# Second attention of a two-layer decoder: the causal mask by GpSimd's selection, and another order of weight preparation and transposes

## Chip, cores and metric

The kernel runs on one core of a Trainium2 chip. The metric is the device time of one execution in microseconds (us). TensorE (PE in the profile) multiplies matrices, VectorE (DVE) and ScalarE (ACT) do elementwise work, GpSimd (POOL) does small jobs, and SyncE (SP) issues the DMAs. A whole run is one launch.

## What is computed

Two decoder layers on 256 tokens of width 1024, in float32. The first layer's mixer is a dilated window attention, the second's is a forgetting attention; each mixer is followed by a SwiGLU layer of width 2816. The change lies in the second mixer:

```python
def forgetting_mixer(h, w_in, b_f, w_out):
    proj = h @ w_in
    q, k, v = ...                      # 16 heads of 64
    log_f = jax.nn.log_sigmoid(proj[..., 3 * ATTN_WIDTH:] + b_f)
    c = lax.cumsum(log_f, axis=1)
    def block(args):                   # 128 queries at a time
        s = jnp.einsum('bihd,bjhd->bhij', qi, k) * scale
        s = s + ci[..., None] - ck[:, :, None, :]
        s = jnp.where(key_pos[None, :] <= qpos[:, None], s, NEG_INF)
        p = jax.nn.softmax(s, axis=-1)
        return jnp.einsum('bhij,bjhd->bihd', p, vf)
    ...
    return o @ w_out
```

## The kernel before

Every weight matrix is streamed from HBM in pieces of 128 x 2048, and used in two parts so that products keep float32 accuracy: a high part `wh` (ScalarE copies the loaded half piece `raw` to a shorter type, L79) and a low part `wl` (VectorE subtracts `wh` from `raw`, L83). Each product is three matmuls (`mm3`, L202 and L207): high times high, high times low, low times high. `raw` has five buffers of half a piece, used in turn, so SyncE can issue a load only when the subtraction five half pieces earlier has read its buffer. `wh` and `wl` have four buffers each. `weights` (L153) is called by the step that uses a piece, and makes the pieces up to two steps ahead.

The second attention (L904 to L974) goes through the twelve pieces of its input projection, in the order of `b_units` (L137). The text calls the i-th of them unit i: units 0 to 2 are values, 3 and 4 are q and k of head group 0, 5 and 6 of group 1, 7 and 8 of group 2, 9 and 10 of group 3, and 11 is the values of group 3. A head group is four heads, worked on as two pairs. Between the units stand the steps of the attention, by a table `due` of times: half numbers mean in the middle of a unit.

- `bias` (L846): loads the rows of cumulated log gates for a pair into all partitions (L849) and adds the causal mask to the two diagonal blocks of each head on GpSimd (L851).
- `scores_b` (L857): q times k on PE into four PSUM banks (L864), then VectorE adds the bias and takes the maximum (L876), ScalarE takes exponentials and their sums (L878), VectorE the reciprocal (L883), and both scale the probabilities `p` (L885 ScalarE, L886 VectorE). In it `release` emits low parts that were held back for units 3 and 5.
- `trans_b` (L889): twelve transposes of `p` on PE (L298) into three PSUM banks, and three copies of these to SBUF on VectorE (L303).
- `pv_b` (L896): values times transposed `p` on PE (L310), then the split of the result into `oth` and `otl`, the high and low part of the attention's output.

For group 0 scores come after unit 5, transposes in the middle of unit 7, values and the scores of group 1 at the end of unit 7's projection. Groups 1 and 2 follow two and four units later, with transposes in the middle of units 9 and 11. Group 3 has its scores at the end of unit 11, and its transposes and values inside the output projection.

`out_proj` (L630) multiplies the attention's output by `b_out`, first for the first 128 tokens (t = 0): for each pair of n (two halves of the width) and k (eight slices) three matmuls, called a piece here. Slices k = 6 and 7 are those of group 3. With `done` = 5 the pieces of slices 0 to 4 are put around the steps that are still due.

Each engine works through its instructions in one order that is fixed when the program is built, from the order of the code, with `first()` (L43) moving an instruction ahead and `issue_after` keeping one behind another. An engine waits at an instruction whose inputs or buffers aren't there, and all that is behind it waits too.

Of the kernel before, what the change touches and what calls it, by code (L numbers as in the profile page):

```python
# [10 lines left out]
F32 = mybir.dt.float32  # L11
F32R = mybir.dt.float32r
AF = mybir.ActivationFunctionType
ALU = mybir.AluOpType
AX = mybir.AxisListType

P = 128
D = 1024
S = 256
KT = D // P  # L20
# [7 lines left out]
NEG = -1e30  # L28
# [3 lines left out]
def trunk(ctx: ExitStack, tc: tile.TileContext, T, out):  # L32
    nc = tc.nc

    cst = ctx.enter_context(tc.tile_pool(name="cst", bufs=1))
# [23 lines left out]
    def const(name, shape):  # L59
        c = cst.tile(shape, F32, name=name)  # L60
        nc.sync.dma_start(c, T[name])
        return c
# [90 lines left out]
    def weights(nm, i, after=None, ahead=AHEAD, hold=None):  # L153

        upto = order.index((nm, i)) + ahead
        while state["next"] <= min(upto, len(order) - 1):
            key = order[state["next"]]
            cuts = []
            ready[key] = piece(key, cuts)
            for cut in cuts:  # L160
                cut(after, hold)
            state["next"] += 1
        return ready.pop((nm, i))
# [91 lines left out]
    def v_tile(o=None, r=None):  # L255

        v = ap.tile([P, 512], F32, tag="v", name="v", bufs=7)
        with first():
            if r:
                for t in range(2):  # L260
                    s = slice(t * S, (t + 1) * S)
                    nc.scalar.activation(v[:, s], o[:, s], AF.Copy, scale=r[t])
            elif o is not None:
                nc.scalar.activation(v, o, AF.Copy)
        return v
# [24 lines left out]
    def masked(s, sc, mask):  # L290
        with first():
            nc.vector.scalar_tensor_tensor(s, sc, HD ** -0.5, mask, op0=ALU.mult, op1=ALU.add)

    def transposed(blocks, copy=nc.vector.tensor_copy, tag="tr", home="pt"):

        tr = psum(tag)
        for i, b in enumerate(blocks):
            nc.tensor.transpose(tr[:, i * P:(i + 1) * P], b, ident)  # L298
        n = len(blocks) * P
        bufs, cols = {"pt": (3, 512), "bias": (4, 6 * P)}[home]  # L300
        w = ap.tile([P, cols], F32, tag=home, name="pt", bufs=bufs)
        with first():
            copy(w[:, :n], tr[:, :n])  # L303
        return w

    def pv(o, v, kb, pr, w, n, start, stop):
# [21 lines left out]
    for i, c in enumerate(room):  # L328
        b = 1 + (i > 1)
        n = S + 512  # L330
# [17 lines left out]
    xt = xt_tile()  # L348
# [15 lines left out]
    part = [sums[:, :S], sums[:, S:512], sums[:, 512:], sqs[:, :512], sqs[:, 512:]]  # L364
# [8 lines left out]
    for k in range(KT):  # L373
        if k % 4 == 0:
            w = tuple(wp.tile([P, 2048], F32R, tag=y, name=y, bufs=4) for y in ("wh", "wl"))
# [49 lines left out]
    x = []  # L425

    ot = fm_tile("ot", KT, 1)
# [102 lines left out]
    due = {}  # L530
# [5 lines left out]
    for i, (hq, g, w) in enumerate(a_units):  # L536
# [15 lines left out]
        if i in (24, 31):  # L552
            x.append(hrow("x"))
            t = len(x) - 1
# [72 lines left out]
                parts.append(sq(hn[:, s]))  # L627
        return hn, parts

    def out_proj(nm, ot, h, grow, done, banks):  # L630

        ws = [weights(nm, i) for i in range(4)]
        xt = xt_tile()
        res = []

        def part(t, acc, nk):
            last = None
            for n, k in nk:
                c = (k % 2) * D + n * 512
                last = mm3(acc[n], both(ot, ALL, k, slice(t * P, (t + 1) * P)),  # L640
                           both(ws[k // 2], ALL, slice(c, c + 512)), k == 0, k == KT - 1)
            return last

        def cols(ks):
            return [(n, k) for n in range(2) for k in ks]

        for t in range(2):
            acc = [psum(banks[t]) for _ in range(2)]
            if t == 0:

                nk = cols(range(done))
                last = part(t, acc, nk[:done])
                nk = nk[done:]
                per = -(-len(nk) // (len(due) - 1))
                for i in sorted(due):
                    with tc.issue_after(last.ins):
                        for fn, a in due[i]:
                            fn(*a)
                    last = part(t, acc, nk[:per]) or last
                    nk = nk[per:]  # L660
                due.clear()
                part(t, acc, nk)
                last = part(t, acc, cols(range(done, KT)))
            else:
                part(t, acc, cols(range(2)))
                with tc.issue_after(last.ins):
                    part(t, acc, cols(range(2, 6)))
                    norm_t(*res[0], grow, xt, 0)
                    part(t, acc, cols(range(6, KT)))
            res.append(residual(acc, h[t], f"h_{nm}{t}"))  # L670
        return res, xt
# [110 lines left out]
        return res  # L782

    g_f = load_grow(1)
    hs, xt = out_proj("a_out", ot, x, g_f, 6, ("sc", "mm"))
    causal = const("causal", [P, P])
    bf = cst.tile([P, NH], F32, name="bf")
    nc.sync.dma_start(bf, T["bf"].partition_broadcast(P))
    wf32 = const("b_f_in", [P, KT * NH]).rearrange("p (k c) -> p k c", k=KT)
# [36 lines left out]
    behind = []  # L826
# [19 lines left out]
    def bias(hq, pr):  # L846

        b = ap.tile([P, 6 * P], F32, tag="bias", name="bias", bufs=4)
        nc.sync.dma_start(b, sums[hq * 4 + pr * 2:hq * 4 + pr * 2 + 2].rearrange("h c -> (h c)").partition_broadcast(P))  # L849
        d = b.rearrange("p (h b j) -> p h b j", h=2, b=3)[:, :, 0:3:2]  # L850
        nc.gpsimd.tensor_tensor(d, d, causal[:, None, None, :].to_broadcast([P, 2, 2, P]), op=ALU.add)  # L851
        bq[hq]["bias", pr] = b

    ot = fm_tile("ot", KT, 1)
# [80 lines left out]
    for i, (hq, w) in enumerate(b_units):  # L935
        if i < 3:
            continue
        wt = weights("b_in", hq * 3 + w, behind if i in (3, 5) else None, hold=held)
        o = psum("mm")
        if w < 2:  # L940
            for c in range(2):
                proj_feat(xt, wt, o[:, c * S:(c + 1) * S], c)
                if c == 0:
                    for fn, a in due.pop(i - 0.5, ()):
                        fn(*a)
            if w == 0:

                for fn, a in due.pop(i, ()):
                    fn(*a)
            bq[hq][w] = ap.tile([P, 2, S], F32, tag=f"fm{w}", name=f"fb{w}", bufs=2)  # L950
            with first():
                held = nc.scalar.activation(bq[hq][w], o.rearrange("p (a b) -> p a b", a=2), AF.Copy,
                                            scale=(0.125, 1.0)[w])
            if w == 1:
                j = i + 1

                later(j, scores_b, hq)
                if hq < 2:
                    for pr in range(2):
                        later(j + 1, bias, hq + 2, pr)  # L960
                later(j + 1.5, trans_b, hq)
                for pr in range(2):
                    later(j + 2, pv_b, hq, pr)
        else:
            for t in range(2):
                proj_tok(xt, wt, o[:, t * S:(t + 1) * S], t)
                if t == 0:
                    for fn, a in due.pop(i - 0.5, ()):
                        fn(*a)
            bq[hq][w] = v_tile(o)  # L970
        for fn, a in due.pop(i, ()):
            fn(*a)
    g_f = load_grow(3)
    hs, xt = out_proj("b_out", ot, [h for h, _ in hs], g_f, 5, ("mm", "sc"))  # L974

    def finish(t, h, parts):
        r = rstd(parts)
# [41 lines left out]
def _constants():  # L1019

    pos = np.arange(S)
    perm = np.array([P * b + 4 * u + a for b in range(2) for a in range(4) for u in range(32)])
    half = ROT // 2
    inv = np.power(np.float32(500000.0), -np.arange(half, dtype=np.float32) * np.float32(2.0) / np.float32(ROT))
    ang = (pos[:, None].astype(np.float32) * inv[None, :].astype(np.float32)).astype(np.float32)
    cos, sin = np.cos(ang)[perm], np.sin(ang)[perm]
    lay = lambda a, fill: np.ascontiguousarray(np.tile(np.concatenate(
        [a.T, np.full((HD - ROT, S), fill)]), (2, 1)).astype(np.float32))
    rcos = lay(np.concatenate([cos, cos], 1), 1.0)
    rsin = lay(np.concatenate([-sin, sin], 1), 0.0)  # L1030
    d = perm[:, None] - perm[None, :]
    bias = lambda ok: np.where(ok, 0.0, NEG).astype(np.float32)
    m0 = bias((d >= 0) & (d <= 128))
    m0 = np.concatenate([m0[:P, :P], m0[P:]], 1)

    res = np.concatenate([np.arange(32), P + np.arange(32)])
    own = np.tile(d[res][:, res].reshape(2, 1, 32, 64), (1, 4, 1, 1)).reshape(2, P, 64)
    m1 = bias((own >= 0) & (own % 4 == 0) & (own <= 512))
    m2 = bias((own >= 0) & (own % 16 == 0) & (own <= 2048))
    m12 = np.stack([m1, m2], 2).transpose(1, 0, 2, 3).reshape(P, S)  # L1040
    causal = bias(pos[:P, None] >= pos[None, :P])
    return perm, {
        "ident": np.eye(P, dtype=np.float32), "rcos": rcos, "rsin": rsin,
        "mask0": m0, "mask12": m12,
        "causal": causal,
    }


# [57 lines left out]
```

## Time and profile before

| | |
|---|---|
| time, three runs | 745.35, 745.67, 746.33 us; median 745.67 us |
| profiled execution | 749.27 us, of which the span of the trace is 747.5 us |
| mean granted TensorE clock | 0.994 |
| DVE, ACT, POOL busy | 66%, 50%, 9% of the span |
| moved by DMA | 138.07 MB, 185 GB/s |
| second attention, units 3 to 11 and the output projection | about 463 to 560 us of the span |

The trace is one execution. A row of the timeline gives the start in us, the length in us, the engine, the line of the kernel, the operation with output and inputs, the count, and in brackets how long the engine had been idle and what released it. A row of the chain gives start, length and what ran there; the chain is followed back from the program's last instruction. In the rows of one line the three numbers are the shortest, the median and the longest duration in ns. Matmuls overlap: their spacing, not their length, is the time that they take on PE.

### The profile page before, as it was taken

What the parts mean: (1) busy time and instruction counts of PE and PEld (TensorE: products, weight loads), DVE (VectorE), ACT (ScalarE), POOL (GpSimd) and SP (SyncE); (2) the same over time, 40 slices, a digit from 0 to 9 for tenths busy, and PEclk for the clock granted to TensorE, in tenths of its full rate; (3) what the DMA queues carried; (4) which work ended last, traced back from release to release, by engine and by line L of the source; (5) the groups of instructions that cost most, each with busy time, mean ns of one, the idle gap of its engine ahead of it and who ended that gap; (6) DMA issues with size and microseconds to landing.
All of it is one profiled execution on the core that took longest, in us unless ns stands there. A gap on an engine that the chain in (4) does not pass through costs nothing.

```text
span 747.5 us, 14342 instructions
## 1 busy us (share of the span) xinstructions
PE 737.5 (99%) x5916; PEld 680.5 (91%) x5916; DVE 492.6 (66%) x768; ACT 375.7 (50%) x617; POOL 66.8 (9%) x98
## 2 busy tenths in 40 slices
PE   9999999999999999999999999999999999999996
PEld 7999989999988789999999988979789999999995
DVE  6997987787888575545455474686767545456533
ACT  7536437437436565344454453576555444444521
POOL 0600003005005000000000004211000000000001
PEclk9999999999999999999999999999999999999998
DMA  8865544644646267565667452874537665656601
GB/s 330 298 203 171 177 155 151 203 159 153 209 144 222 82 229 238 191 200 179 202 204 241 138 168 87 288 243 146 171 105 221 231 198 180 202 189 215 209 1 56
DMA packets 39441, 138.07 MB, mean 185 GB/s; under 512 B 4528, under 2 KB 5840, under 8 KB 39376
## 3 DMA queue, kind: packets, MB, share of 16 engines
q1 hardware_dynamic: 39232, 137.01, 55.3%
q8 instruction: 46, 0.75, 0.4%
q14 instruction: 19, 0.16, 0.1%
q10 hardware_dynamic: 144, 0.15, 0.1%
HBM read 136.07 MB, written 1.07 MB: 183 GB/s over the span
## 4 chain that ended last, share of the span: by engine, by line
PE 90%; ACT 3%; DMA 3%; DVE 2%; issue 1%; SPq 0%; POOL 0%; POOLq 0%; DVEq 0%; ACTq 0%
PE ps_mm L207 31%; PE ps_mm L202 16%; PE ps_tr L207 9%; PE ps_sc L207 8%; PE ps_o L207 7%; PE ps_tr L202 5%; PE ps_sc L202 4%; PE ps_o L202 4%; PE ps_o L310 2%; DMA raw<-in_b_in 2%; DVE wl L83 1%; DMA otl<-in_lead 1%; PE ps_tr L298 1%; ACT wh L79 1%; PE ps_sc L473 1%; ACT p L878 1%
## 5 line engine op out<-in xcount | busy, mean ns | idle before, releaser
L79 ACT ACTIVATE wh<-raw 128x1024 fp32r<-128x1024 f32 x236 | 243.2, 1055 | 240.4 <-PE ps_tr L207 66.5
L83 DVE TENSOR_TENSOR wl<-raw,wh 128x1024 fp32r<-128x1024 f32 x236 | 288.5, 1242 | 88.1 <-ACT wh L79 87.8
L202 PE MATMUL ps_mm<-xt,wh 128*128 128x256 f32 x816 | 228.2, 280 | 0.0
L207 PE MATMUL ps_mm<-xt,wl 128*128 128x256 f32 x816 | 226.8, 278 | 0.1
L207 PE MATMUL ps_mm<-xt,wh 128*128 128x256 f32 x816 | 226.6, 278 | 0.0
L202 PEld LDWEIGHTS ps_mm<-xt,wh 128*128 128x128 f32 x816 | 153.9, 189 | 1.8 <-issue 1.7
L207 PEld LDWEIGHTS ps_mm<-xt,wl 128*128 128x128 f32 x816 | 153.4, 188 | 0.5 <-DVE wl L83 0.5
L207 PEld LDWEIGHTS ps_mm<-xt,wh 128*128 128x128 f32 x816 | 153.4, 188 | 0.0
L207 PE MATMUL ps_tr<-xt,wl 128*128 128x256 f32 x304 | 83.8, 276 | 0.0
L207 PE MATMUL ps_tr<-xt,wh 128*128 128x256 f32 x304 | 83.8, 276 | 0.0
L202 PE MATMUL ps_tr<-xt,wh 128*128 128x256 f32 x304 | 83.6, 276 | 0.0
L702 DVE TENSOR_TENSOR sa<-ps_tr,sa 128x256 f32<-128x256 f32 x38 | 16.1, 424 | 73.9 <-PE ps_tr L207 73.8
L207 PEld LDWEIGHTS ps_tr<-xt,wh 128*128 128x128 f32 x304 | 57.1, 188 | 0.0
L207 PEld LDWEIGHTS ps_tr<-xt,wl 128*128 128x128 f32 x304 | 57.1, 188 | 0.0
L202 PEld LDWEIGHTS ps_tr<-xt,wh 128*128 128x128 f32 x304 | 56.9, 188 | 0.0
L284 POOL COPY v<-v 32x256 f32<-32x256 f32 x64 | 38.0, 594 | 176.1 <-ACT v L280 173.4
L202 PE MATMUL ps_mm<-wh,xt 128*128 128x512 f32 (+1 forms) x144 | 49.8, 346 | 0.0
L207 PE MATMUL ps_mm<-wl,xt 128*128 128x512 f32 (+1 forms) x149 | 49.1, 335 | 0.0
L207 PE MATMUL ps_mm<-wh,xt 128*128 128x512 f32 (+1 forms) x149 | 49.1, 335 | 0.0
L172 POOL TENSOR_SCALAR rs<-ssq 128x1 f32<-128x1 f32 x7 | 2.1, 303 | 422.8 <-ACT junk L181 422.8
L202 PE MATMUL ps_sc<-wh,ah 128*128 128x512 f32 x80 | 31.4, 392 | 0.0
L207 PE MATMUL ps_sc<-wl,ah 128*128 128x512 f32 (+1 forms) x82 | 31.3, 385 | 0.0
(230 smaller groups left out, 1103.3 us busy)
## 6 DMA issues: line engine op xcount, KB each, us to landing
raw<-in_gu SPq DMA_DIRECT2D x88, 512.0 KB, 4.8
raw<-in_a_in SPq DMA_DIRECT2D x68, 512.0 KB, 4.6
raw<-in_dn SPq DMA_DIRECT2D x44, 512.0 KB, 4.6
raw<-in_b_in SPq DMA_DIRECT2D x24, 512.0 KB, 4.7
raw<-in_a_out SPq DMA_DIRECT2D x8, 512.0 KB, 5.3
raw<-in_b_out SPq DMA_DIRECT2D x8, 512.0 KB, 4.9
bias<-sums SPq DMA_DIRECT2D x8, 384.0 KB, 6.1
grow<-in_norms SPq DMA_DIRECT2D x4, 512.0 KB, 5.9
```

Of the source, the lines that this page charges most:

```text
L79: a = nc.scalar.activation(view(hi), src, AF.Copy)
L83: return nc.vector.tensor_tensor(view(lo), src, view(hi).bitcast(F32), op=ALU.subtract)
L172: nc.gpsimd.tensor_scalar(m, s, rest, None, op0=ALU.add)
L202: nc.tensor.matmul(o, sh, mh, start=start, stop=False)
L207: last = nc.tensor.matmul(o[:, u], s, m[:, u], start=False, stop=end and u.stop == n)
L284: nc.gpsimd.tensor_copy(v[1 + a % 2][n:n + 32, a // 2 * S:a // 2 * S + S], by_t[a * 32:a * 32 + 32, t, g])
L298: nc.tensor.transpose(tr[:, i * P:(i + 1) * P], b, ident)
L310: nc.tensor.matmul(o[h * HD:(h + 1) * HD], v[:, c:c + HD], w(h), start=start, stop=stop)
L473: nc.tensor.matmul(sc[h][c, o:o + 64], q[HR[h], pr, qb * P + a * 32:qb * P + a * 32 + 32], k[HR[h], pr].rearrange("p (b n) -> p b n", b=2) ...
L702: nc.vector.tensor_tensor(a, u, sg, op=ALU.mult)
L878: nc.scalar.activation(s[:, u], s[:, u], AF.Exp, bias=nm[:, j:j + 1], scale=-1.0, accum_out=den[:, j:j + 1])
```

## The change

Three edits. The mask of the diagonal blocks is made by GpSimd's `affine_select`, which keeps an element where row minus column is at least 0 and writes -1e30 elsewhere, two instructions for a pair's bias (one for each block of 128 queries) in place of one addition; the constant `causal` and its load are gone, and an unused tile keeps its place. In units 7, 9 and 11, in the middle of which a group is transposed, the low parts of the pieces made there (two half pieces each) are emitted behind the group's last copy. And in the output projection `out_proj` puts nine pieces of slices 0 to 5 ahead of the last transposes, where five of slices 0 to 4 stood.

```diff
+    copied = {}
+
     def transposed(blocks, copy=nc.vector.tensor_copy, tag="tr", home="pt"):
...
         with first():
-            copy(w[:, :n], tr[:, :n])
+            copied["last"] = copy(w[:, :n], tr[:, :n])
         return w
...
-    def out_proj(nm, ot, h, grow, done, banks):
+    def out_proj(nm, ot, h, grow, ks, done, banks):
...
-                nk = cols(range(done))
+                nk = cols(range(ks))
                 last = part(t, acc, nk[:done])
                 nk = nk[done:]
...
-                last = part(t, acc, cols(range(done, KT)))
+                last = part(t, acc, cols(range(ks, KT)))
...
-    hs, xt = out_proj("a_out", ot, x, g_f, 6, ("sc", "mm"))
-    causal = const("causal", [P, P])
+    hs, xt = out_proj("a_out", ot, x, g_f, 6, 6, ("sc", "mm"))
+    cst.tile([P, P], F32, name="gap")
...
         d = b.rearrange("p (h b j) -> p h b j", h=2, b=3)[:, :, 0:3:2]
-        nc.gpsimd.tensor_tensor(d, d, causal[:, None, None, :].to_broadcast([P, 2, 2, P]), op=ALU.add)
+        for e in range(2):
+            nc.gpsimd.affine_select(d[:, :, e], d[:, :, e], [[0, 2], [-1, P]], ALU.is_ge, NEG, base=0,
+                                    channel_multiplier=1)
...
-        wt = weights("b_in", hq * 3 + w, behind if i in (3, 5) else None, hold=held)
+        lows = [] if any(fn is trans_b for fn, _ in due.get(i - 0.5, ())) else None
+        wt = weights("b_in", hq * 3 + w, behind if i in (3, 5) else lows, hold=held)
...
                 if c == 0:
                     for fn, a in due.pop(i - 0.5, ()):
                         fn(*a)
+                    for low in lows or ():
+                        low(copied["last"])
...
-    hs, xt = out_proj("b_out", ot, [h for h, _ in hs], g_f, 5, ("mm", "sc"))
+    hs, xt = out_proj("b_out", ot, [h for h, _ in hs], g_f, 6, 9, ("mm", "sc"))
```

The same two lines with `low(copied["last"])` stand in the branch of the value units. Three places show how the instructions move. First VectorE's order in the middle of unit 7, around the copies of group 0 (`p` are its probabilities, `pt` their transposes; the numbers of lines shift by up to nine), before:

```order
L886 TENSOR_SCALAR p<-p,c_b 128x256 x2
L83 TENSOR_TENSOR wl<-raw,wh 128x1024 x3
L303 COPY pt<-ps_tr 128x512 x2
L303 COPY pt<-ps_o 128x512
L83 TENSOR_TENSOR wl<-raw,wh 128x1024
L83 TENSOR_TENSOR otl<-ps_o,oth 128x256 x2
```

and in the changed kernel:

```order
L890 TENSOR_SCALAR p<-p,c_b 128x256 x2
L83 TENSOR_TENSOR wl<-raw,wh 128x1024
L305 COPY pt<-ps_tr 128x512 x2
L305 COPY pt<-ps_o 128x512
L83 TENSOR_TENSOR wl<-raw,wh 128x1024 x3
L83 TENSOR_TENSOR otl<-ps_o,oth 128x256 x2
```

Two subtractions, the low parts of unit 9's weights, went from ahead of the copies to behind them. In units 9 and 11 two go behind in the same way. The second place is VectorE's order at the last group, from the reciprocals in `scores_b` to the copies inside the output projection, before:

```order
L883 RECIPROCAL c_b<-den_b 128x4
L83 TENSOR_TENSOR wl<-raw,wh 128x1024
L886 TENSOR_SCALAR p<-p,c_b 128x256 x2
L883 RECIPROCAL c_b<-den_b 128x4
L303 COPY pt<-ps_tr 128x512
L886 TENSOR_SCALAR p<-p,c_b 128x256 x2
L303 COPY pt<-ps_tr 128x512
L303 COPY pt<-ps_o 128x512
```

and in the changed kernel:

```order
L887 RECIPROCAL c_b<-den_b 128x4
L83 TENSOR_TENSOR wl<-raw,wh 128x1024
L890 TENSOR_SCALAR p<-p,c_b 128x256 x2
L83 TENSOR_TENSOR wl<-raw,wh 128x1024
L887 RECIPROCAL c_b<-den_b 128x4
L890 TENSOR_SCALAR p<-p,c_b 128x256 x2
L305 COPY pt<-ps_tr 128x512 x2
L305 COPY pt<-ps_o 128x512
```

One subtraction more stands ahead of the second reciprocal, and no copy stands ahead of the last scaling. The third place is PE in the output projection, from the end of its fifth piece to the end of its seventh, before:

```order
L207 MATMUL ps_mm<-wh,otl 128x512
L298 MATMUL ps_tr<-ident,p 128x128
L202 MATMUL ps_mm<-wh,oth 128x512
L298 MATMUL ps_tr<-ident,p 128x128 x5
L207 MATMUL ps_mm<-wl,oth 128x512
L207 MATMUL ps_mm<-wh,otl 128x512
L298 MATMUL ps_o<-ident,p 128x128
L202 MATMUL ps_mm<-wh,oth 128x512
L207 MATMUL ps_mm<-wl,oth 128x512
L298 MATMUL ps_tr<-ident,p 128x128 x2
L298 MATMUL ps_o<-ident,p 128x128 x3
L207 MATMUL ps_mm<-wh,otl 128x512
```

and in the changed kernel, from the end of its ninth piece on:

```order
L207 MATMUL ps_mm<-wh,otl 128x512
L300 MATMUL ps_tr<-ident,p 128x128 x8
L300 MATMUL ps_o<-ident,p 128x128 x4
L202 MATMUL ps_mm<-wh,oth 128x512
L207 MATMUL ps_mm<-wl,oth 128x512
```

The twelve transposes stand in one block behind nine pieces instead of among the matmuls of pieces six and seven. Three pieces follow, then the values, then four pieces of slices 6 and 7. Orders on ScalarE are the same in both kernels; on GpSimd sixteen selections stand where eight additions stood, and on SyncE only the load of `causal` is gone.

More of the change, by code (lines that the diff above doesn't have):

```diff
@@ L969, in trunk @@
                         fn(*a)
+                    for low in lows or ():
+                        low(copied["last"])
             bq[hq][w] = v_tile(o)
@@ L1040, in _constants @@
     m12 = np.stack([m1, m2], 2).transpose(1, 0, 2, 3).reshape(P, S)
-    causal = bias(pos[:P, None] >= pos[None, :P])
     return perm, {
@@ L1044, in _constants @@
         "mask0": m0, "mask12": m12,
-        "causal": causal,
     }
```

## Prediction

> **What bounds the kernel now.** I read the page's busy times, then the waits of PE, then two stretches in time.
>
> ```profile
> PE 737.5 (99%) x5916; PEld 680.5 (91%) x5916; DVE 492.6 (66%) x768; ACT 375.7 (50%) x617; POOL 66.8 (9%) x98
> PE ps_o L310 <- DVE pt L303: 1.8, 2, 1.6
> PE ps_tr L298 <- ACT p L885: 0.2, 1, 0.2
> 493.80:495.40 1.60, 0.02 (x2) 1.00 0.76 243
> 495.40:500.50 5.10, 4.94 (x32) 0.67 0.85 292
> ```
>
> The columns of the last two rows are stretch, length, PE busy, PEclk, DMA share, GB/s. PE is the bound, so an edit off PE is worth only what it takes out of PE's holes. In the second attention PE waits twice, and both waits belong to steps that the change moves: 1.8 us for the copies of L303, and 0.2 us for the scaled `p`. Behind the first PE runs at a granted clock of 0.67 for 5.1 us. The rest of the program is gapless PE work, which this change leaves as it is.
>
> **The first place, unit 7 (q of head group 2).** The chain of waits shows the hole, and beside it the same steps one head group later, undisturbed:
>
> ```profile
> 494.72 1.81 DVE pt L303 x3
> 496.57 1.44 PE ps_o L310 x8
> 498.01 1.58 PE ps_sc L864 x8
> 499.59 0.98 PE ps_tr L864 x8
> ...
> 513.30 1.45 PE ps_o L310 x16
> 514.75 0.86 PE ps_sc L864 x8
> 515.60 0.66 PE ps_tr L864 x8
> ```
>
> ```profile
> 493.51 0.28 PE L207 MATMUL ps_mm<-xt,wl 128*128 128x256 f32 x1
> 495.38 0.93 PE L310 MATMUL ps_o<-pt,v 128*64 128x256 f32 x6 [1.59 <-DVE pt L303]
> 528.51 0.28 PE L207 MATMUL ps_mm<-wh,xt 128*128 128x256 f32 x1
> 528.72 1.52 PE L310 MATMUL ps_o<-pt,v 128*64 128x256 f32 x16
> ```
>
> Undisturbed, values and scores take 515.60 + 0.66 - 513.30 = 2.96 us, and start 0.21 us after the projection's last matmul started (528.51 to 528.72). Here they should have begun at 493.72 and ended at 496.68; unit 8 began at 499.59 + 0.98 = 500.57. The loss is **3.9 us**. Of it about 1.75 us is half clock: the last 8 values matmuls and the scores took 4.0 us (496.57 to 500.57) where half of 1.45 plus 0.86 and 0.66 is 2.25. The copies were late because of what VectorE had ahead of them:
>
> ```profile
> 490.13 4.58 DVE L83 TENSOR_TENSOR wl<-raw,wh 128x1024 fp32r<-128x1024 f32 x3
> 494.64 1.27 DVE L303 COPY pt<-ps_tr 128x512 f32<-128x512 f32 x2
> 490.13 2.32 DVE L83 TENSOR_TENSOR wl<-raw,wh 128x1024 fp32r<-128x1024 f32 x1
> ```
>
> Three subtractions run from 490.13 to 494.71; the first ends at 490.13 + 2.32 = 492.45. In the new order only that one is ahead. The copies then start at 492.4 and end at 493.05, 493.65 and 494.3 (two in 1.27, three in 1.81). The values need the first two at 493.72 and the third half-way, at 494.45. So the hole closes, with 0.15 us to spare at the tightest. I count **3.8 us** off PE, one tenth being left for a late third copy.
>
> The two subtractions that go behind the copies (unit 9's weights) run from 494.3 on, with the fourth that stood there already: three at 1.2 us (the median below) end at 497.9. Behind them and two short ones of the values stand the reads of the scores:
>
> ```profile
> 499.73 0.29 DVE L876 CUSTOM_DVE_ANT_0 p<-ps_sc,bias 128x128 f32<-128x128 f32 x1 [0.84 <-PE ps_sc L864]
> 504.51 0.62 DVE L886 TENSOR_SCALAR p<-p,c_b 128x256 f32<-128x256 f32 x2
> 509.25 0.87 PE ps_tr L298 x8
> 510.12 0.44 PE ps_o L298 x4
> ```
>
> They move only from 499.73 to about 498.6, since VectorE and not PE now holds them, while PE moves by 3.8. The second group's `p` is ready at 505.13 - 1.1 = 504.0, and its transposes come at 509.25 - 3.8 = 505.45: 1.4 us are left of what were 4.1. That cover, a unit and a half of projection, hides it; were it gone, each tenth would be PE's. Unit 9, whose weights these are, begins two thirds of the way from 500.57 to 509.25, now at 502.6, 5 us after their subtraction. At the second and third groups moving the copies up gives PE nothing: both waits for L303 in the first rows, 1.59 and 0.16, lie in the first group.
>
> **The second place, the output projection.** The first four rows show today's loss, the others why I expect one to stay:
>
> ```profile
> 531.68 0.50 PE L202 MATMUL ps_mm<-wh,oth 128*128 128x512 f32 x1
> 535.62 0.33 PE L298 MATMUL ps_tr<-ident,p 128*128 128x128 f32 x1 [0.24 <-ACT p L885]
> 541.01 1.30 PE L310 MATMUL ps_o<-pt,v 128*64 128x256 f32 x12
> 546.38 0.45 PE ps_mm L207 x2
> 523.66 2.36 DVE L83 TENSOR_TENSOR wl<-raw,wh 128x1024 fp32r<-128x1024 f32 x2 [1.54 <-ACT wh L79]
> 524.91 0.33 SPq L100 DMA_DIRECT2D raw<-in_b_out  x1
> raw<-in_b_out SPq DMA_DIRECT2D x1, 512.0 KB, 5.1
> raw<-in_b_out SPq DMA_DIRECT2D x3, 512.0 KB, 3.6
> 524.64 0.87 PE ps_tr L298 x8
> 530.79 1.07 ACT L79 ACTIVATE wh<-raw 128x1024 fp32r<-128x1024 f32 x1
> 532.53 0.40 ACT L878 ACTIVATE p<-p,nm_b 128x128 f32<-128x128 f32 x1 [0.67 <-DVE nm_b L876]
> 537.45 0.61 DVE L886 TENSOR_SCALAR p<-p,c_b 128x256 f32<-128x256 f32 x2
> ```
>
> From 531.68 to 541.01 PE passes ten pieces of three matmuls at 0.685 (two in 0.45, from the row at 546.38) and twelve transposes, 0.87 + 0.44: 6.85 + 1.31 + 0.15 for the changes of kind = 8.3 of 9.33. Today 1.0 us is lost, as single transposes of the last group come early and wait. In the new order nine pieces come first: with 531.68 moved to 527.9, the transposes are due at 527.9 + 0.1 + 9 x 0.685 = 534.15.
>
> Is `p` there? The last half weight of `b_out` is loaded into the buffer that the first subtraction at 523.66 frees (its end, 524.87, and the issue at 524.91 show that), and its copy on ScalarE, 530.79 today, stands ahead of the last group's exponentials at 532.53. That subtraction now goes behind the third group's copies. These start half-way through transposes that begin at 524.64 - 3.8 = 520.8, so at 521.3, and end 1.9 later, at 523.2; the subtraction ends at 524.35. So this load moves by 0.55 us while PE moves by 3.8. It lands 5.1 us later, at 529.5; the copy ends at 530.6, and the exponentials begin there, 1.9 us before today's 532.53 and not 3.8. Today the last scaled `p` is done at 538.06, 5.5 us after they begin; that gives 536.1. The extra subtraction ahead of the last reciprocal can add up to its own 1.2 us, or nothing, as the reciprocal waits for ScalarE's exponentials too; I add 0.1, since in the rows of PE's waits it is ScalarE that ends last. PE can do six of the twelve transposes, to 534.8, before it needs the second pair's `p`, and then waits about **1.4 us**. Against the 1.0 lost today this place is a loss of 0.4. Its bounds: no wait at all if the load lands in 3.6 us, the median of the last three of `b_out` (1.0 gained); and 1.1 more than taken if the subtraction counts in full.
>
> **The mask.**
>
> ```profile
> L851 POOL TENSOR_TENSOR bias<-bias,causal x8: 1276/1297/1337, 476.9 to 507.2; 128x512 f32<-128x512 f32 x8
> L284 POOL COPY v<-v x64: 391/397/1466, 26.4 to 239.2; 32x256 f32<-32x256 f32 x64
> L83 DVE TENSOR_TENSOR wl<-raw,wh x24: 1187/1212/2316, 466.4 to 534.5; 128x1024 fp32r<-128x1024 f32 x24
> 486.58 1.29 POOL L851 TENSOR_TENSOR bias<-bias,causal 128x512 f32<-128x512 f32 x1 [3.98 <-DMA bias<-sums]
> 490.03 1.34 POOL L851 TENSOR_TENSOR bias<-bias,causal 128x512 f32<-128x512 f32 x1 [2.16 <-DVE p L886]
> ```
>
> Eight additions of 1.30 us go, sixteen selections of 256 elements per partition come. No selection is in the trace. The nearest row is GpSimd's copy, one input and as many elements per partition, 0.39 us at least and 1.47 at most; I take 0.5, so 1.0 for a pair where 1.30 stood. What matters is VectorE: a subtraction that meets an addition (490.13 beside 490.03) takes 2.32 instead of 1.21, so it stands still about as long as GpSimd works. At 0.5 that is 0.3 shorter each time, which I don't count. At 1.47 a pair lasts 1.64 longer, twice in a row ahead of the first transposes and copies, which takes back 2 x 1.64 - 0.7 of slack = 2.6 us. The lost constant load is 64 KB in a stretch where PE waits for nothing: 0.
>
> [...]
>
> **Sum.** On the profiled execution: -3.8 + 0.4 = -3.4, from 749.27 to 745.9. The median of the timed runs, 745.67, is 3.6 under that execution. One profile can't tell whether every execution pays the half clock behind so short a hole; I take half of its 1.75. So 745.67 - (3.8 - 0.9) + 0.4 = **743.1**. The steps carry to the end: the two rows at the top are all of PE's waits behind the first microseconds, and the later loads go into buffers that PE's progress frees. About 0.2% (1.5 us) is what can be told from no change: 744.2 and 747.2.
>
> **Rivals.**
> - As forecast: chance 0.55, 741.9 to 744.1 as the half clock is or isn't in the timed runs.
> - The wait returns in the output projection with a half clock of its own. For it: 1.4 us of idle is near the 1.6 that had one. Against: the 0.24 us hole there had none, and PE has 128-wide work around it. 743.1 + 1.75 = 744.85, no change; 0.20.
> - The last `b_out` load lands early (3.6 us), and no wait is left: 743.1 - 1.4 = 741.7; 0.13.
> - Slower: a dear selection. GpSimd holds VectorE from 486.58 and from 490.03, in front of the first group's transposes and copies. At s us each it costs 2 x (2s - 1.3) - 0.7, which eats the gain of 2.5 at s = 1.45; at s = 2.0 it is 4.7, and the time 743.1 + 4.7 = 747.8. Against it: no GpSimd row of 256 elements is above 1.47. 0.12. [...]
>
> That the move doesn't happen is excluded by the rows of the instruction order.
>
> Range 741.2 to 746.0: down to the third case, up to the selection's bound of 1.47 (743.1 + 2.6 = 745.7). Faster 0.68, same 0.20, slower 0.12.
>
> **What would show it.** The copies after the first transposes start by 492.6 and no PE row carries a wait for L303 there; the half clock at 496 is gone. ScalarE waits for the load of `b_out` before the last exponentials, and PE for `p` by 1 to 2 us in the output projection. The selections' rows say 0.4 to 0.7. Wrong would be: selections over 1.3, a wait for weights in units 8 to 11, or transposes of the second group that wait for `p`.

## The result, and the profile after

The changed kernel takes 742.78 us (median of five runs, 741.92 to 743.09); the kernel before, run beside it, 746.11 us (745.35 to 748.07). The ratio is 0.9953, with a 95% interval of 0.9937 to 0.9968: faster by 3.3 us. The forecast was 743.1. Its sign and size held, but two of its terms were off by more than a microsecond each, in opposite directions; most of what follows is about these.

The changed kernel's profiled execution took 742.78 us, span 741.0. First PE's busy time and, from the waits, all that PE waits for over 0.15 us:

```profile
PE 733.1 (99%) x5916; PEld 679.1 (92%) x5916; DVE 489.5 (66%) x768; ACT 375.5 (51%) x617; POOL 65.0 (9%) x106
PE ps_o L321 <- DVE mhalf L65: 0.9, 1, 0.9
```

The one wait left is in the first microseconds of the program. Both waits of the second attention, 1.8 us for copies and 0.2 us for `p`, are gone. The chain of waits at the first group (start, length, what ran):

```profile
488.20 0.87 PE ps_tr L300 x8
489.07 0.44 PE ps_o L300 x4
...
492.25 1.45 PE ps_o L312 x16
493.70 0.86 PE ps_sc L868 x8
494.55 0.66 PE ps_tr L868 x8
```

Values and scores now take 2.96 us in one piece (494.55 + 0.66 - 492.25), the undisturbed length that the prediction took from the later group. VectorE's timeline shows why:

```profile
487.60 1.23 DVE L83 TENSOR_TENSOR wl<-raw,wh 128x1024 fp32r<-128x1024 f32 x1 [0.43 <-ACT wh L79]
488.75 1.28 DVE L305 COPY pt<-ps_tr 128x512 f32<-128x512 f32 x2
489.95 0.68 DVE L305 COPY pt<-ps_o 128x512 f32<-128x512 f32 x1
490.55 2.35 DVE L83 TENSOR_TENSOR wl<-raw,wh 128x1024 fp32r<-128x1024 f32 x2
```

One subtraction is ahead of the copies, and the last copy ends at 490.63, 1.6 us before the values start.

### Where one execution differs from another

One profile of each kernel is not enough here, since the program's first 470 us vary by up to 2.4 us, nearly as much as the change is worth: PE's 3950th matmul, ahead of everything that the change moves on PE, came between 468.07 and 470.44 us in fourteen profiles, with no clear order among the kernels. So I counted PE's matmuls in each trace and took two stretches: A from the 4100th to the 4250th (unit 7 with the first group's transposes, values and the next scores), and B from the 4450th to the 4550th (the output projection around the last group). The same work of PE lies between these counts in every kernel but for its order, so a stretch is longer only where PE waits, sets its matmuls wider apart, or runs at half clock.

```
                                    A       B     us
kernel before, first profile      20.81   17.74
kernel before, second profile     18.37   17.74
low parts behind copies alone     16.62   17.87
output projection alone           18.08   16.82
selection alone                   18.22   17.77
changed kernel                    16.62   16.79
changed, low parts as before      18.80   16.79
changed, output proj. as before   16.62   17.70
changed, mask by addition         16.86   16.79
```

From the 4550th matmul to the last one all nine lie within 192.73 to 193.03. The table already says most: A belongs to the low parts, B to the output projection, and the first profile of the kernel before was an unusual execution: its 749.27 us lie above all other times of that kernel (744.48 to 748.07). In the second profile its time was 746.33 (median 746.48 of 29 runs beside it), and these are its waits and the place:

```profile
PE ps_o L310 <- DVE pt L303: 1.0, 2, 0.9
PE ps_tr L298 <- ACT p L885: 0.2, 1, 0.2
...
485.16 2.30 POOL L851 TENSOR_TENSOR bias<-bias,causal 128x512 f32<-128x512 f32 x1 [4.14 <-DMA bias<-sums]
488.62 2.28 POOL L851 TENSOR_TENSOR bias<-bias,causal 128x512 f32<-128x512 f32 x1 [1.16 <-DVE p L886]
488.52 1.22 DVE L83 TENSOR_TENSOR wl<-raw,wh 128x1024 fp32r<-128x1024 f32 x1
490.30 2.81 DVE L83 TENSOR_TENSOR wl<-raw,wh 128x1024 fp32r<-128x1024 f32 x2 [0.56 <-ACT wh L79]
```

Here the subtraction started first (488.52) and GpSimd's addition, 0.1 us behind it, took 2.28 us in place of 1.30. In the first profile the addition started at 490.03, 0.1 us ahead, and the subtraction took 2.32. Both times it was the second to start that took longer, by 0.98 us beside the addition's median of 1.30 and by 1.11 beside the subtraction's of 1.21. The prediction's picture, in which VectorE always stands still, fits only one of the two. In the second profile PE waits 0.88 and 0.16 us for the copies, and no half clock follows. These two waits are 1.04 of the 1.75 us by which A is longer than in the changed kernel; 0.46 more lie in wider spacing of the matmuls around them, and 0.24 in the matmuls of the next unit, which no view explains.

### The profile page after: what moved, and what is told of

The parts are those of the page before. It is cut to its first block, busy times and chain, and to the rows that moved or that the text cites. A ratio compares the mean times of both kernels' runs of the same rounds, so it can differ in the third digit from the quotient of the medians.

```text
span 741.0 us, 14364 instructions
## 1 busy us (share of the span) xinstructions
PE 733.1 (99%) x5916; PEld 679.1 (92%) x5916; DVE 489.5 (66%) x768; ACT 375.5 (51%) x617; POOL 65.0 (9%) x106
## 3 DMA queue, kind: packets, MB, share of 16 engines
HBM read 136.00 MB, written 1.07 MB: 185 GB/s over the span
## 4 chain that ended last, share of the span: by engine, by line
PE 96%; ACT 1%; DMA 1%; DVE 1%; issue 0%; SPq 0%; POOL 0%; POOLq 0%; DVEq 0%; ACTq 0%
PE ps_mm L207 34%; PE ps_mm L202 17%; PE ps_tr L207 9%; PE ps_sc L207 8%; PE ps_o L207 7%; PE ps_tr L202 5%; PE ps_sc L202 4%; PE ps_o L202 4%; PE ps_o L312 2%; PE ps_tr L300 1%; DMA otl<-in_lead 1%; PE ps_sc L475 1%; PE ps_tr L195 1%; PE ps_o L300 1%; PE ps_sc L868 0%; PE ps_sc L457 0%
## 5 line engine op out<-in xcount | busy, mean ns | idle before, releaser
L83 DVE TENSOR_TENSOR wl<-raw,wh 128x1024 fp32r<-128x1024 f32 x236 | 285.1, 1228 | 82.7 <-ACT wh L79 82.4
```

The source lines that it names most:

```text
L83: return nc.vector.tensor_tensor(view(lo), src, view(hi).bitcast(F32), op=ALU.subtract)
```

## Experiments

Twelve kernels ran in three batches, five rounds each, with the kernel before beside them (746.48, 745.44 and 745.75 us). "Order theory" says that the time comes from the place of the copies and transposes in the engines' orders; "port theory" (only a name here, no run shows a port) says that it comes from GpSimd no longer holding VectorE.

**The kernel before once more, and each of the three edits alone.** The three edits, each made by itself:

```diff
+        lows = [] if any(fn is trans_b for fn, _ in due.get(i - 0.5, ())) else None
-        wt = weights("b_in", hq * 3 + w, behind if i in (3, 5) else None, hold=held)
+        wt = weights("b_in", hq * 3 + w, behind if i in (3, 5) else lows, hold=held)
...
+                    for low in lows or ():
+                        low(copied["last"])
```

```diff
-    hs, xt = out_proj("b_out", ot, [h for h, _ in hs], g_f, 5, ("mm", "sc"))
+    hs, xt = out_proj("b_out", ot, [h for h, _ in hs], g_f, 6, 9, ("mm", "sc"))
```

```diff
-        nc.gpsimd.tensor_tensor(d, d, causal[:, None, None, :].to_broadcast([P, 2, 2, P]), op=ALU.add)
+        for e in range(2):
+            nc.gpsimd.affine_select(d[:, :, e], d[:, :, e], [[0, 2], [-1, P]], ALU.is_ge, NEG, base=0,
+                                    channel_multiplier=1)
```

> The kernel before, unchanged, for a second profile. If its profiled execution was a usual one: the half clock of 3.4 us behind the first values matmuls again, PE waiting about 1.6 us for the copies, and a span near 747. If that execution was an unusual one: the wait of 1.6 us again (it follows from VectorE's order), but full clock behind it, and a span 1.7 us and more below 747. The difference of 1.3 us that the two profiles show ahead of the second attention's first scores should then be there too, between two profiles of one kernel. Timed: ratio 1.000.

> Only the low parts go behind the copies; mask by addition, old output projection. Order theory (the copies were late because three subtractions stood ahead): PE's wait for the copies of the first group goes, 1.6 to 1.8 us and the half clock behind it with it, copies start about 2.3 us before they did; time 2 to 3.5 us down. The output projection keeps its loss or gets worse, as the load of the last half weight is later against PE. Port theory (they were late because VectorE stood still beside GpSimd's additions): the hole goes here too, as only one held-up subtraction is left ahead; the two theories differ in the run with the selection alone.

> Only the nine pieces of slices 0 to 5 ahead of the last transposes. The first group's wait of 1.6 us stays. In the output projection the transposes come 6.3 us after its first matmul, when the last scaled probabilities are there (6.4 us after it in the old trace): no wait of PE, 0.9 to 1.0 us less from the first piece to the first values; time 0.9 us down. If the old loss there was not from the early transposes: no difference.

> Only the mask by selection. Order theory: the three subtractions stay ahead of the first copies, so PE's wait stays at 1.0 us or more, and the time changes by less than 0.7 us. Port theory: subtractions beside selections take 1.2 instead of 2.3 us, so the third ends 1.6 us earlier, PE's wait falls to 0.0 to 0.4 us, the half clock goes with it, and the time falls by 2 to 3 us: nearly as much as with the low parts moved.

| kernel | us | ratio to before | 95% interval |
|---|---|---|---|
| before again | 746.33 | 1.0000 | 0.9991 to 1.0009 |
| low parts alone | 744.38 | 0.9969 | 0.9958 to 0.9980 |
| output projection alone | 745.48 | 0.9988 | 0.9979 to 0.9997 |
| selection alone | 745.79 | 0.9988 | 0.9979 to 0.9996 |

The second profile of the kernel before had neither the half clock nor the wait of 1.6 us that was expected of it either way; 0.88 us is what it showed. Low parts alone close the hole (A 16.62). With the selection alone it stays, although no subtraction takes over 1.38 us any more. Its row in PE's waits, and the two subtractions ahead of the copies:

```profile
PE ps_o L310 <- DVE pt L303: 1.1, 2, 1.0
489.08 1.24 DVE L83 TENSOR_TENSOR wl<-raw,wh 128x1024 fp32r<-128x1024 f32 x1 [0.55 <-ACT wh L79]
491.10 1.23 DVE L83 TENSOR_TENSOR wl<-raw,wh 128x1024 fp32r<-128x1024 f32 x1 [0.77 <-ACT wh L79]
```

VectorE is free earlier, and waits 0.55 and 0.77 us for ScalarE's `wh` instead: ScalarE ends last. So port theory falls as the account of the gain at the copies. Nor are the 0.9 us that the timed runs give to the selection alone in A of this trace (A 18.22, against 18.08 in the kernel with the output projection alone, which has the old addition and the old order there).

**Each edit left out of the changed kernel**, by taking back one of the three diffs above.

> Selections and the new output projection, but the low parts ahead of the copies as before. Order theory: the hole ahead of the first group's values is back at 1.0 to 1.2 us plus 0.16, and the stretch from the first scores to unit 8 is 1.5 to 1.7 us longer than in the changed kernel; 1.5 to 1.7 us slower than the changed kernel, ratio about 0.9980 to 0.9985. Port theory (selections alone close the hole by freeing VectorE): within 0.5 of the changed kernel, ratio 0.996.

> Selections and low parts behind the copies, but the output projection as before (five pieces of slices 0 to 4 ahead of the last transposes). By the single parts (low parts alone -2.3, output projection alone -0.9, selection alone -0.9 with nothing in its trace): 0.9 us slower than the changed kernel, about 743.6 to 743.9, with one PE wait for p of about 0.7 us in the output projection. If the parts overlap (the output projection's gain comes out only when PE is late elsewhere): within 0.3 of the changed kernel.

> Low parts behind the copies and the new output projection, but the mask by the old addition. Order theory (the mask is worth nothing to the time): the same as the changed kernel, about 742.8 to 743.3, ratio 0.9955 to 0.996, no PE wait for copies and none for p. Port theory (the selection frees VectorE and so is a part of the gain; alone it measured 0.9 us): about 743.7, ratio 0.9968, with a PE wait somewhere in units 7 to 11 that the changed kernel has not.

| changed kernel, but | us | ratio to before | 95% interval |
|---|---|---|---|
| low parts as before | 744.00 | 0.9978 | 0.9969 to 0.9987 |
| output projection as before | 743.91 | 0.9979 | 0.9970 to 0.9988 |
| mask by addition | 743.07 | 0.9970 | 0.9958 to 0.9981 |

Without the low parts the hole is back:

```profile
PE ps_o L310 <- DVE pt L303: 1.4, 2, 1.3
489.23 1.23 DVE L83 TENSOR_TENSOR wl<-raw,wh 128x1024 fp32r<-128x1024 f32 x1 [0.56 <-ACT wh L79]
491.25 2.36 DVE L83 TENSOR_TENSOR wl<-raw,wh 128x1024 fp32r<-128x1024 f32 x2 [0.79 <-ACT wh L79]
```

Without the new output projection PE's transposes of the last group are torn apart again and wait for `p`, and B is 0.91 us longer:

```profile
530.27 0.33 PE L300 MATMUL ps_tr<-ident,p 128*128 128x128 f32 x1 [0.53 <-ACT p L889]
530.69 0.81 PE L300 MATMUL ps_tr<-ident,p 128*128 128x128 f32 x5
533.41 0.38 PE L300 MATMUL ps_tr<-ident,p 128*128 128x128 f32 x2
```

With the addition nothing but 0.24 us in A comes back, among the first group's transposes. The timed ratio, 0.9970, lies above the 0.9953, 0.9963 and 0.9961 of three kernels with the changed order (below), but the intervals overlap. Order theory carries the low parts and the output projection; whether the selection is worth half a microsecond in the timed runs stays open. The sizes agree less well than the places. Against the changed order beside them (742.96 and 742.38 us, below), the median is 1.0 us longer without the low parts, where 1.5 to 1.7 were expected and A shows 2.2, and 1.5 longer without the new output projection, where 0.9 were expected and B shows 0.91. A's 2.2 comes from the slowest of that kernel's eleven executions (745.26 us).

**Dearer selections.** The selections done four times, and twice:

```diff
-        for e in range(2):
+        for e in (0, 0, 0, 0, 1, 1, 1, 1):
```

> The changed kernel with each selection done four times over (the repeats leave the values as they are), so that a pair's mask takes GpSimd about 3.3 us where it took 0.81 and the old addition 1.30. Rival of the prediction (VectorE stands still as long as GpSimd works): subtractions beside a selection last 2 to 4 us, twice in a row ahead of the first transposes and copies, a loss of about 2 x (3.3 - 1.3) - 0.7 = 3.3 us, time about 746, with PE waits for the copies of 1.5 us or more in units 7 or 9. Order theory, with selections that never hold VectorE: subtractions stay at 1.2 to 1.4 us, selections that meet one stretch, the bias is ready 2.5 us later than in the changed kernel but still units ahead of the scores that read it, time 742.8 within 0.5.

> The changed kernel with each selection done twice (the repeats leave the values as they are): 1.62 us for a pair. In the run with four, ten selections of five pairs stood back to back on GpSimd for 14.4 us, and a subtraction that came in their midst lasted 9.97 us, until the last of them. Queue theory (VectorE is held from when it meets a running selection until GpSimd first has a gap): at 1.62 us a pair each is done before the next pair's bias has landed, so no subtraction lasts over 3 us, PE waits for nothing, and the time is that of the changed kernel within 0.4, ratio about 0.9960. Proportional theory (each us of GpSimd beside VectorE costs as much): a third of the loss of the run with four, 2.3 us slower than the changed kernel, ratio about 0.9990.

Four times: 749.79 us, ratio 1.0061 (1.0048 to 1.0073), 7 us slower than the changed kernel and worse than either expectation. GpSimd's row, the first subtraction that met it, and PE:

```profile
475.46 14.40 POOL L854 TENSOR_SCALAR_AFFINE_SELECT bias<-bias 128x256 f32<-128x256 f32 x40 [15.09 <-DMA bias<-sums]
480.96 9.97 DVE L83 TENSOR_TENSOR wl<-raw,wh 128x1024 fp32r<-128x1024 f32 x1
490.99 0.58 PE L207 MATMUL ps_mm<-xt,wl 128*128 128x256 f32 x1 [4.54 <-DVE wl L83]
490.90:494.30 3.40, 3.31 (x15) 3.31 (x16) 3.40 (x12) 2.86 (x11) 0.00 (x0) 0.50 0.51 166
```

The forty selections of the first five pairs (forty, not the ten of the second expectation) stood back to back on GpSimd, 0.36 us each. A subtraction that began in their midst ended 1.07 us after the last of them (489.86), about a subtraction's own length, as if it had got nothing done until then. PE ran out of weights for 4.54 us, and then went at half clock (the 0.50 in the last row's PEclk). So selections can hold VectorE. But later in the same execution three subtractions met eight selections in a row, and came in between them:

```profile
497.60 5.87 POOL L854 TENSOR_SCALAR_AFFINE_SELECT bias<-bias 128x256 f32<-128x256 f32 x8 [7.74 <-DMA bias<-sums]
498.49 3.99 DVE L83 TENSOR_TENSOR wl<-raw,wh 128x1024 fp32r<-128x1024 f32 x3
```

In the changed kernel it is the selections that wait. Its rows in the whole stretch, and the two pairs that met a subtraction there:

```profile
L854 POOL TENSOR_SCALAR_AFFINE_SELECT bias<-bias x16: 406/407/1429, 474.5 to 503.9; 128x256 f32<-128x256 f32 x16
L83 DVE TENSOR_TENSOR wl<-raw,wh x18: 1195/1218/1232, 480.1 to 530.9; 128x1024 fp32r<-128x1024 f32 x18
484.44 1.84 POOL L854 TENSOR_SCALAR_AFFINE_SELECT bias<-bias 128x256 f32<-128x256 f32 x2 [4.87 <-DMA bias<-sums]
487.35 1.75 POOL L854 TENSOR_SCALAR_AFFINE_SELECT bias<-bias 128x256 f32<-128x256 f32 x2 [1.06 <-DMA bias<-sums]
```

The pairs were stretched from 0.77 to 1.84 and 1.75 us, and no subtraction took over 1.23.

Twice: 743.26 us, ratio 0.9966 (0.9954 to 0.9978), PE waits for nothing, A 16.62. As queue theory expected, the time is that of the changed kernel; the proportional theory's 2.3 us are not there. But queue theory's mechanism did not hold:

```profile
487.51 2.52 POOL L854 TENSOR_SCALAR_AFFINE_SELECT bias<-bias 128x256 f32<-128x256 f32 x4 [0.15 <-DMA bias<-sums]
488.01 1.39 DVE L83 TENSOR_TENSOR wl<-raw,wh 128x1024 fp32r<-128x1024 f32 x1
```

Four selections need 1.48 us undisturbed. This subtraction met them half-way and took 1.39, while they took 2.52: it came in between two of them. Why VectorE got in there and among the eight, and not among the forty, no run tells.

**A later load for the output projection.** The prediction's wait of 1.4 us rested on the last half weight of `b_out`. Two kernels were to delay its load by turning round two subtractions of unit 11, the first by emitting them in the other order, the second by tying one behind the other:

```diff
-                    for low in lows or ():
+                    for low in reversed(lows or []):
                         low(copied["last"])
```

```diff
-                    for low in lows or ():
-                        low(copied["last"])
+                    if lows:
+                        lows[0](lows[1](copied["last"]))
```

> The changed kernel with one thing turned round: the two low parts held back in unit 11 are emitted in the other order, so the raw buffer that takes the last half weight of b_out is read 1.2 us later. Load theory (the last exponentials, and with them the last scaled p and the last six transposes, are set by the landing of that load): issue of the load 1.2 us later (523.7 where the changed kernel had 522.5), ScalarE's wait for it 2.2 us in place of 1.07, exponentials, last scaled p 1.2 us later, PE waits about 1.0 to 1.2 us for p inside the output projection (none in the changed kernel), time about 743.9 against 742.8, ratio to the kernel before 0.9967. Rival (the exponentials are set by VectorE's maxima and the load is hidden): no PE wait over 0.2, time 742.8, ratio 0.9953.

> The run late_load was meant to hold back the last load of b_out, but turning round the emission of the two low parts left VectorE's order as it was, so that run is the changed kernel once more. Here the first of the two low parts of unit 11 is tied behind the second, so VectorE does them in the other order and the buffer for that load comes free 1.2 us later. Load theory: the load's issue, ScalarE's wait for it (2.1 to 2.3 us in place of 1.07), the last exponentials (2.4 us behind the start of the output projection in place of 1.2) and the last scaled p all move by 1.2 us; PE waits 1.0 to 1.2 us for p between the transposes; the output projection up to the values of the last group takes 10.9 us in place of 9.83; ratio about 0.9975. Rival (the load is hidden, VectorE's maxima set the exponentials): no PE wait over 0.2, ratio 0.9955 to 0.9965 as in the changed kernel.

Neither delayed it. In the instruction lists of both kernels the two subtractions have changed places (the second expectation is wrong on the first kernel), but the last load of `b_out` has changed its buffer with them: it takes the one that comes free first, and not that of the half piece five earlier. So the five buffers of `raw` aren't strictly used in turn. In the second kernel the load was issued 0.02 us behind the end of the first of the four subtractions (521.45 + 1.22 = 522.67):

```profile
521.45 1.22 DVE L83 TENSOR_TENSOR wl<-raw,wh 128x1024 fp32r<-128x1024 f32 x1
522.69 0.33 SPq L100 DMA_DIRECT2D raw<-in_b_out  x1
526.37 1.06 ACT L79 ACTIVATE wh<-raw 128x1024 fp32r<-128x1024 f32 x1 [0.94 <-DMA raw<-in_b_out]
```

So in time they are two more runs of the changed kernel: 742.38 us, ratio 0.9963 (0.9950 to 0.9975), and 742.96, ratio 0.9961 (0.9949 to 0.9974), with no wait of PE in either. What a late load would cost was not tried.

**A longer hole.** The kernel before, with the first copy of the first group done twice:

```diff
         with first():
+            if long.pop("hole", None):
+                copy(w[:, :n], tr[:, :n])
             copy(w[:, :n], tr[:, :n])
```

> The kernel before with the first copy of the first group's transposes done twice, so the copies that the values wait for come 0.62 us later: a hole of about 1.6 us, as in the first profile of the kernel before, in place of the 1.0 of its second. If an idle of 1.6 us sets off the half clock each time: a stretch of granted clock 0.5 of about 3.4 us behind the hole, and 0.6 + 1.75 = 2.4 us slower than the kernel before, ratio 1.003. If that half clock was an accident of one execution: no half clock behind the hole, 0.6 us slower, ratio 1.0008.

The median of eleven executions is 747.99 us; one of them took 1230.93, and without it the median is 747.39. The ratio without it is 1.0024 (1.0015 to 1.0033), between the two expectations, and the single times tell why: five executions took 746.40 to 746.79, and five 747.99 to 749.29. The profiled one, 748.21, is of the upper five:

```profile
488.38 4.58 DVE L83 TENSOR_TENSOR wl<-raw,wh 128x1024 fp32r<-128x1024 f32 x3
494.81 1.84 PE L314 MATMUL ps_o<-pt,v 128*64 128x256 f32 x16 [2.44 <-DVE pt L307]
495.87:499.28 3.41, 3.41 (x24) 2.29 (x18) 2.28 (x10) 2.14 (x6) 0.00 (x0) 0.50 0.71 256
```

Here the addition held the first subtraction (4.58 for three), the hole was 2.44 us and not 1.6, and 3.41 us at half clock followed it. The medians of the two fives are 746.47 and 748.41, 1.9 us apart, near the 1.75 that the prediction gave to the half clock. That the lower five had none is inferred from their times; no profile shows one of them. They may also have had a shorter hole, with the subtraction ahead of the addition as in the second profile of the kernel before.

The traces do show when the half clock comes. In all fourteen, every change of the granted clock lies a whole number of 3.413 us behind the trace's first change to full clock: at 144 of them in the first profile of the kernel before (5.20 to 496.72) and here (4.35 to 495.87), at 142 with the selections done four times (6.23 to 490.93). In these traces the clock thus went by a grid of 3.413 us, whose start lay between 4.3 and 6.3 us after the program's (4.35 to 6.23 in the three named) and differed from execution to execution. These are the steps of the grid just ahead of the half clock in these three profiles, and then the steps with the hole in two that had no half clock, the second profile of the kernel before and the changed kernel with the low parts as before (stretch, length, PE busy and its instructions, PEclk, DMA share, GB/s):

```profile
493.31:496.72 3.41, 1.66 (x15) 1.00 0.67 219
492.46:495.87 3.41, 1.06 (x12) 1.00 0.88 294
487.51:490.93 3.42, 0.00 (x0) 1.00 0.00 0
492.63:496.05 3.42, 2.38 (x23) 1.00 0.67 198
492.83:496.24 3.41, 2.00 (x18) 1.00 0.66 226
```

In the fourteen traces, with the ends of the program, half clock came after every step at full clock in which PE was busy for 1.66 us or less (1.53 at the end of the first profile of the kernel before, 1.06 at that of the changed kernel), and after none in which it was busy for 2.00 or more. So neither "each time" nor "an accident" says it: in these traces it went by how much of a hole fell into one step. The first profile's hole of 1.59 and 0.16 us lay in a single step and left PE busy for 1.66; the usual one, 0.88 and 0.16, leaves at least 3.41 - 1.04 = 2.37 us, wherever it falls, and by these figures is too short. That the lower five of the ten had their hole split by a step's end, or had a shorter one, was not seen.

## Why the prediction was right, step by step

- **First place, mechanism: right.** The copies start at once behind one subtraction, no PE row waits for them, values and scores take 2.96 us, and the half clock is gone. Against the first profile of the kernel before, A is 4.19 us shorter, near the 3.8 that was forecast. The copies had 1.6 us to spare where the prediction gave 0.15 (its own times give less, 493.65 against 493.72 for the first two); one reason is that the subtraction ahead of them wasn't held and took 1.23 us in place of 2.32.
- **First place, size in the timed runs: too large.** The forecast took 2.9 us, as half of the half clock's 1.75 and the whole hole of that profile. Against the second profile, whose time is that of the median, A is 1.75 shorter (18.37 to 16.62). So by that profile the usual loss there is 1.75 us, without half clock, and not the 3.9 that the first one showed. The step that failed is the transfer from one execution to the median: the first profile's execution was 2.9 us longer than the second's, and 2.4 of these were this very place (20.81 against 18.37), 0.8 its start (469.74 against 468.96), with 0.3 the other way in the rest.
- **Cover of the second group: right.** Its scaled `p` ended 2.4 us ahead of its transposes in the changed kernel (501.06 and 503.43), where 1.4 were forecast.
- **Output projection: wrong in sign.** +0.4 was forecast, B shows -0.95 (17.74 to 16.79). The mis-sized term is the load of the last half weight:

```profile
raw<-in_b_out SPq DMA_DIRECT2D x1, 512.0 KB, 3.8
526.33 1.06 ACT L79 ACTIVATE wh<-raw 128x1024 fp32r<-128x1024 f32 x1 [1.07 <-DMA raw<-in_b_out]
527.29 0.39 ACT L882 ACTIVATE p<-p,nm_b 128x128 f32<-128x128 f32 x1
532.25 0.62 DVE L890 TENSOR_SCALAR p<-p,c_b 128x256 f32<-128x256 f32 x2
```

  ScalarE does wait for it, 1.07 us, and the last `p` is ready 5.6 us behind the first exponential, where 5.6 was taken. But the load lands 3.8 us after its issue and not 5.1; the exponentials start 1.27 us behind the output projection (526.02) and not 2.7, and the transposes, due at 532.29, need no wait. There is nothing to spare: the last `p` ends at 532.87, as the seventh transpose comes. The rival with the early load, given 0.13, is what happened at this place. With 5.1 in its place the last `p` would have come 1.3 us later and PE would have waited about 1.2 us (worked out from these rows, not run). The 5.1 was one execution's: in the six profiles with the low parts as before this load took 3.7 to 5.1 us (4.8 in the second profile of the kernel before), and in the eight with the low parts behind the copies 3.7 to 3.9. Why it varies is open.
- **The two errors cancel, by luck.** In usual executions the two places give -1.75 and -0.95, together -2.7; the forecast had -2.9 and +0.4. That 743.1 came within 0.4 us of the measured 742.78 is no sign that its terms were right. The timed -3.3 has an interval of -4.7 to -2.4 us, and the two other runs of this order give -2.8 and -2.9.
- **Mask: right in cost, wrong in picture.** A selection takes 0.41 us where 0.5 was taken, and the subtractions are no longer stretched. That this frees VectorE but not the copies, since ScalarE then ends last, was not seen. The dear selection was no case here, but with four times the work it did hold VectorE; the prediction's formula would give 3.3 us for that, and the kernel lost 7.
- **Half clock in the output projection:** not tested, since no wait arose there. By the rows of the longer hole, 1.4 us of waiting would have left PE busy for about 2.0 us of a step of 3.41, and a step with 2.00 brought no half clock.

## What to carry to other kernels

Work that nobody waits for soon belongs behind the copy that PE waits for next, and in the fixed order here that was worth more than making the engine that held it up faster. Where the profiled execution lies far from the median of the timed runs, look first for what is unusual in it, in the very stretch that the change touches, and take a second profile of the same kernel before sizing a term. Take a DMA's duration from more than one execution, since one and the same load took 3.7 to 5.1 us here, and when an edit speeds one engine up, ask which engine ends last then.

## What was not expected of the hardware

- VectorE's subtraction and GpSimd's addition held each other up in order of start: in the first profile of the kernel before the addition started 0.1 us ahead, and the subtraction took 2.32 us where its median is 1.21; in the second the subtraction started 0.1 us ahead, and the addition took 2.28 where its median is 1.30. A row of forty selections kept one subtraction of 1.2 us waiting for 8.9 us, though subtractions came in among a row of eight.
- The half clock came as one stretch of 3.41 us in each of the profiles that had it in the middle, behind 1.59, 2.44 and 4.54 us of waiting, not behind 0.9 or 1.3. In the fourteen traces the clock changed only on a grid of 3.413 us. Half clock came behind the steps of it in which PE was busy for 1.66, 1.06 and 0.00 us, and not behind those with 2.00 and 2.38.
